# Two transformer layers on one core: some early loads moved to GpSimd's queue, the first products taken by parts, and products of zeros at two places

## The chip, the cores and the metric

The kernel runs on one core of one Trainium2 chip. TensorE (PE) multiplies, VectorE (DVE) and ScalarE (ACT) do the elementwise work, GpSimd (POOL) computes one small power per norm and issues some loads, SyncE (SP) issues nearly all loads. The metric is the device time of one execution in microseconds, the median over several runs.

## The reference

Two layers act on x, 256 rows of 1024 float32 values. A layer is a half-weighted SwiGLU block, a mixer with three kinds of attention, and a second half-weighted SwiGLU block. Each stage begins with an RMS norm, and one more norm ends the program.

```python
for l in range(DEPTH):
    x = x + 0.5 * swiglu(rms_norm(x, ffn1_norm[l]), ffn1_w_gate[l], ffn1_w_up[l], ffn1_w_down[l])
    x = x + hybrid_mixer(rms_norm(x, mix_norm[l]), w_in[l], ...)
    x = x + 0.5 * swiglu(rms_norm(x, ffn2_norm[l]), ffn2_w_gate[l], ffn2_w_up[l], ffn2_w_down[l])
return rms_norm(x, final_norm)
```

D_FF is 2816, so a SwiGLU block reads three matrices of 1024 by 2816 values. Here the stages are called f1_0, mx_0, f2_0, f1_1, mx_1 and f2_1.

## The kernel before, in words

**Products.** Every float32 operand is split into a high and a low part (`split`, `high` on ACT, `low` on DVE), and one product is three matmuls: high by high, low by high, high by low (`mm3`, L173). A weight therefore travels: a load into the raw ring `w_r` (or a tile of its own), a copy by ACT into `w_h`, a subtraction by DVE into `w_l`, then the matmuls.

**The order of the work.** The program's order on PE, ACT and DVE is fixed by hand (`ORDERED`): the code advances a clock of its own (`spend`), defers pieces of work by so many microseconds (`defer`), and `need` runs the deferred pieces until a named one is done. An instruction that waits holds everything behind it on its engine. SP and POOL are not in that list: on them the framework's scheduler places the DMAs, and may take one ahead of another that has to wait.

**Loads.** `load` (L313) starts one load and defers its split. The first block of a SwiGLU stage needs two loads of gate and two of up (512 KB each, columns 0 to 255). Then come single blocks of 128 columns: gate block 2 and up block 2 are the first of them (512 KB each, `128x8x128` in the order's rows). The last 1536 columns are done as two units by Strassen-like products G and U with steps 1, 5, 6, 3, 7, 2, 4; their raw quarters (768 KB each, `128x4x384`, tiles `f_G_r` and `f_U_r`, issued at L322) are called G1, G5, G6, G2 and U1 below after the step that loads them. Some quarters are added to a tile already there by a DMA on POOL's queue (L331).

**The start.** Nine matmuls of zeros into a bank `heat` run first (L1185). Then x's first 128 rows (t=0) are normed: ACT sums squares (L429), POOL takes the power -1/2 (L436), DVE scales (L450), PE transposes, DVE multiplies by the gain (L471), ACT and DVE split the result into `f_Th` and `f_Tl`. `first_block` (L574) multiplies t=0 by gate, then by up, then t=1 by both. `second` loads and norms t=1 meanwhile. `opened` loads the tables `rot` and `tab` (64 and 896 KB), which the mixer reads much later.

**Between stages.** The norm of the next stage works per half of the rows. In f1_1, the products of t=0 run while t=1 is being normed; then PE transposes t=1 (`turn`, L456).

Of the kernel before, what the change touches and what calls it, by code (L numbers as in the profile page):

```python
# [13 lines left out]
ALU = mybir.AluOpType  # L14
# [96 lines left out]
def block_kernel(ctx: ExitStack, tc: tile.TileContext, a: dict, c: dict, out: bass.AP):  # L111
# [57 lines left out]
    def transpose(o, src, n=P):  # L169
        nc.tensor.transpose(o, src, ident[:n, :n])  # L170
        spend(0.11)

    def mm3(o, st, mv, first, last, again=False):  # L173

        (sh, sl), (mh, ml) = st, mv
        nc.tensor.matmul(o, sh, mh, start=first, stop=False, skip_group_check=again)  # L176
        nc.tensor.matmul(o, sl, mh, start=False, stop=False, skip_group_check=again)  # L177
        nc.tensor.matmul(o, sh, ml, start=False, stop=last, skip_group_check=again)  # L178
        spend(3 * (max(256, o.shape[-1]) / 2400 + 0.003))
        load_some()  # L180
        while later and later[0][0] <= clock[0]:
            heapq.heappop(later)[2]()
# [125 lines left out]
        of.append([j])  # L308
        return pool.tile(shape, F32, tag=tag, name=name, bufs=bufs), of[-1]

    unit_pool, unit_open = [None], [False]

    def load(j, ring):  # L313
        job = jobs[j]
        name, n = job["name"], job["n"]
        adds = []
        if "unit" in job:
            places, new, add, source, more = job["unit"]
            if new:
                tag, src = new  # L320
                places[tag] = raw_place("raw" + tag, unit_pool[0], 2 if tag == "a" else 1, [P, 4 * UC], f"{name}_r", j)
                nc.sync.dma_start(places[tag][0].rearrange("p (k n) -> p k n", k=4), src)  # L322
            for t in {source, *(add or ()), *(more or ())[:1]}:
                for i in places[t][1]:
                    if i in loaded:
                        loaded[i][2]()
                if places[t][1][-1] != j:
                    places[t][1].append(j)
            if more:
                tag, src = more  # L330
                nc.gpsimd.dma_start(places[tag][0].rearrange("p (k n) -> p k n", k=4), src, accum_op=ALU.add)  # L331
            raw = places[source][0]
            if add:
                to, other = [places[t][0] for t in add]
                adds = [(to, other)]
        else:
            o, old = take(raws, n, j)
            for i in old:
                loaded[i][2]()
            raw = raws["tile"][:, o:o + n]  # L340
            o = 0
            for w, k0, k1, c0, m in job["runs"]:
                e = o + (k1 - k0) * m
                nc.sync.dma_start(raw[:, o:e].rearrange("p (k n) -> p k n", k=k1 - k0),
                                  w[k0 * P:k1 * P, c0:c0 + m].rearrange("(k p) n -> p k n", p=P))
                o = e
        o, _ = take(rings[ring], n, j)
        hi, lo = [rings[ring][i][:, o:o + n] for i in ("hi", "lo")]
        piece = n // 2 if adds else n if job["whole"] else PIECE
        cuts = [(o, min(n, o + piece)) for o in range(0, n, piece)]  # L350
        todo = [lambda o=o, e=e: nc.vector.tensor_tensor(to[:, o:e], to[:, o:e], other[:, o:e], op=ALU.add)  # L351
                for to, other in adds for o, e in cuts]
        todo += [lambda o=o, e=e: high(hi[:, o:e], raw[:, o:e]) for o, e in cuts]
        todo += [lambda o=o, e=e: low(lo[:, o:e], raw[:, o:e], hi[:, o:e]) for o, e in cuts]
        total = len(todo)

        def until(m):
            while len(todo) > m:
                todo.pop(0)()

        size = piece / 1200 + 0.1
        for m in range(total - 1, -1, -1):
            defer(size * (total - 1 - m), lambda m=m: until(m))
        until(total - 1)
        loaded[j] = hi, lo, lambda: until(0), ring
        return SUM if adds else SPLIT if "unit" in job else PACE * n
# [35 lines left out]
        tl = const.tile([P, KT, S], F32R, tag="xTl", name=f"{name}_Tl")  # L402
        return th, tl

    def norm(name, gain_src, last=None, gain_cols=None):


        st = {}
# [30 lines left out]
        def scaled(t):  # L439
            xs, ss, r = st[t]  # L440
            if last is not None:
                xg = st["xg", t]
                nc.scalar.mul(xg[:, half_cols(0)], xg[:, half_cols(0)], r)
                nc.vector.tensor_scalar(xg[:, half_cols(1)], xg[:, half_cols(1)], r, None, op0=ALU.mult)
                for h in (1, 0):
                    last(t, h, xg)
                return
            for h in range(2):
                if gain_cols is not None:
                    nc.vector.tensor_scalar(xs[:, half_cols(h)], x[t][:, half_cols(h)], r, None, op0=ALU.mult)  # L450
                else:
                    nc.vector.scalar_tensor_tensor(xs[:, half_cols(h)], x[t][:, half_cols(h)], r, st["g"][h], op0=ALU.mult, op1=ALU.mult)
                defer(0.8 + 0.7 * h, lambda h=h: turn(t, h))
            made.add((name, t, "rows"))

        def turn(t, h):  # L456
            tp = tp_bank(f"{name}_tp{t}{h}")
            for k in range(4):
                kk = h * 4 + k
                transpose(tp[:, k, :], st[t][0][:, kk * P:(kk + 1) * P])  # L460
            defer(0.3, lambda: parts_of(t, h, tp))

        def parts_of(t, h, tp):
            th, tl = nT[name]
            src = tp
            if name[0] == "f":
                if h == 0:
                    kept[name, t] = row_tile(f"{name}_xr{t}").rearrange("p (k s) -> p k s", s=P)
                if gain_cols is not None:
                    src = kept[name, t][:, h * 4:h * 4 + 4, :]  # L470
                    nc.vector.tensor_tensor(src, tp, gain_cols[:, h * 4:h * 4 + 4, None].to_broadcast([P, 4, P]), op=ALU.mult)  # L471
                    made.add((name, "kept", t, h))
            split(th[:, h * 4:h * 4 + 4, rows(t)], tl[:, h * 4:h * 4 + 4, rows(t)], src)
            if name[0] == "f" and gain_cols is None:
                defer(1.5, lambda: (nc.scalar.activation(kept[name, t][:, h * 4:h * 4 + 4, :], tp, AF.Copy), made.add((name, "kept", t, h))))
            made.add((name, t, h))
            if t == 1 and h == 1:
                table(AF.Exp if name.startswith("mx") else AF.Silu)
# [52 lines left out]
    def ffn(name, done, opening=None, opened=None):  # L531
        xTh, xTl = nT[name]
        steps, tail, f_first = ffn_steps()
        with ExitStack() as ctx2:
# [24 lines left out]
            def glu(g, u, nm, then, key):  # L559
# [11 lines left out]

                defer(0.25, silu)

            def first_block():  # L574

                pair = hidden(0, 2)
                for t in range(NT):
                    ab = acc_bank(f"{name}_b0{t}").rearrange("p (a b) -> p a b", a=2)
                    for i in range(2):
                        for k in range(KT):  # L580
                            need((name, t, k // 4))
                            mm3(ab[:, i, :], (xTh[:, k, rows(t)], xTl[:, k, rows(t)]), part(f"{name}_{'gu'[i]}0", k),
                                k == 0, k == KT - 1)
                        if opening and t == 0 and i == 0:
                            opening()
                        if t and not i:
                            tps[1], unit_open[0] = True, True
                            sums()
# [6 lines left out]
                                            made.update((name, "hT", i, t) for i in range(2))))  # L595

                    glu(ab[:, 0, :], ab[:, 1, :], f"{name}_b0{t}", lambda h, t=t: defer(2.5, lambda: turn(t, h)), (name, "h", 0, t))
                if opening:
                    opened()

            single = {}

# [120 lines left out]

            first_block()
            for step in steps:
                if step[0] == "P":
                    unit_product(*step[1:])
                elif step[0] == "B":
                    block(*step[1:])
                else:  # L730
                    for t in range(NT):
                        for h in range(2):
                            down(step[1], t, h)
# [8 lines left out]
                        down(f, t, h)  # L742
                    defer(0.2, lambda t=t, h=h: update(t, h))
            need((name, "updated"))
            unit_open[0] = False

    def rows_out(name, st, keys, scale, done):

# [432 lines left out]
    nc.scalar.dma_start(gain_rows, a["ffn1_norm"][0].rearrange("(k p) -> k p", p=P))  # L1181
    nc.scalar.dma_start(ident, c["eye"])
    table(AF.Square)
    heat = acc_bank("heat")
    for _ in range(WARM):  # L1185
        nc.tensor.matmul(heat[:, :256], zeros[:, :P], zeros, start=True, stop=True)
    gain_bank = tp_bank("gain_tp")
    transpose(gain_bank[:, 0, :KT], gain_rows, KT)
    gain_cols = small.tile([P, KT], F32, tag="gc", name="gain_cols", bufs=1)
# [2 lines left out]
    first(0, 0)  # L1192
    first(0, 1)
    need(("f1_0", 0, "rows"))
    load(queues[0].pop(0), 0)
    need(("f1_0", 0, 0), ("f1_0", 0, 1))

    def second():
        x_in(1)
# [5 lines left out]
        pace[0] = clock[0]  # L1205

    def opened():
        nc.sync.dma_start(rot, c["rot"])
        nc.sync.dma_start(tab, c["tab"])

    def write(t, h, rows_):
        (nc.scalar, nc.sync)[h].dma_start(out[0, rows(t), half_cols(h)], rows_[:, half_cols(h)])
# [2 lines left out]
    for i, (kind, l) in enumerate(layers):  # L1215
        if i + 1 < len(layers):
            k2, l2 = layers[i + 1]
            done = norm(f"{k2}_{l2}", a[norms[k2]][l2])
        else:
            done = norm("last", a["final_norm"], last=write)  # L1220
        if kind == "mx":
# [35 lines left out]
```

## Time and profile before

| | |
|---|---|
| median of 3 runs | 1272.26 us (1272.09 to 1272.71) |
| the profiled execution | 1275.12 us, of which the span is 1273.3 us |
| PE busy | 1254.1 us, 98% of the span |
| DVE, ACT, POOL busy | 913.9, 748.1 and 55.6 us |
| HBM read | 244.85 MB, 193 GB/s over the span |

The profiled execution is 2.9 us longer than the median. PE is busy nearly all the time, so the places to read are the few at which it waits, and the stretches in which its clock was granted at half speed (1.2 instead of 2.4 GHz). DMA shares above 1.00 in a stretch occur because a packet's time counts where it starts.

### The profile page before, as it was taken

How to read it: one execution, taken by the hardware profiler on the slowest of the kernel's cores; microseconds unless marked ns; L12 is line 12 of the kernel's file. 1: busy time of each engine (PE TensorE's matmuls, PEld its weight loads, DVE VectorE, ACT ScalarE, POOL GpSimd, SP SyncE). 2: the span in 40 equal slices, each digit the busy share in tenths (PEclk: the TensorE clock that was granted, in tenths of full speed). 3: DMA queues.
4: the chain of work that ended last, by engine and by line, in shares of the span. 5: the costliest groups of instructions: out<-in, count | busy, mean ns of one | idle time of the engine just before them, and what ended most of it. 6: DMA issues, size and time to landing. Idle time of an engine off the chain costs nothing.

```text
span 1273.3 us, 21204 instructions
## 1 busy us (share of the span) xinstructions
PE 1254.1 (98%) x8287; PEld 1178.7 (93%) x8287; DVE 913.9 (72%) x1359; ACT 748.1 (59%) x1263; POOL 55.6 (4%) x54
## 2 busy tenths in 40 slices
PE   7999999999999999999999999999999999999997
PEld 6999988999999899999889999899999998999996
DVE  5988767765546868887688877667655577788774
ACT  5665646655556456665466565467655554665652
POOL 0000001000000000000000000000000000000000
PEclk8999999999999999999999999999999999999999
DMA  9997856545435688986589985565464466799762
GB/s 301 259 263 207 225 189 172 153 131 145 127 111 169 208 256 221 267 229 174 165 261 261 247 239 151 168 178 154 134 165 115 135 198 199 215 267 242 221 167 79
DMA packets 206308, 247.28 MB, mean 194 GB/s; under 512 B 7160, under 2 KB 190208, under 8 KB 206208
## 3 DMA queue, kind: packets, MB, share of 16 engines
q1 hardware_dynamic: 188864, 220.16, 56.1%
q0 software_dynamic: 16896, 25.17, 12.1%
q8 instruction: 65, 1.06, 0.3%
q10 hardware_dynamic: 448, 0.59, 0.1%
q14 instruction: 35, 0.29, 0.1%
HBM read 244.85 MB, written 1.05 MB: 193 GB/s over the span
## 4 chain that ended last, share of the span: by engine, by line
PE 94%; DVE 3%; ACT 1%; DMA 1%; issue 0%; POOL 0%; POOLq 0%; ACTq 0%; DVEq 0%
PE f_a L178 6%; PE f_a L177 6%; PE f_a L176 6%; PE f_s L176 6%; PE f_s L177 6%; PE f_s L178 6%; PE f_b L177 6%; PE f_b L178 6%; PE f_b L176 6%; PE mx_ogate L176 4%; PE mx_ogate L178 3%; PE mx_ogate L177 3%; PE mx_odqk L176 2%; PE mx_odqk L177 2%; PE mx_odqk L178 2%; PE mx_sbdil L846 1%
## 5 line engine op out<-in xcount | busy, mean ns | idle before, releaser
L188 DVE TENSOR_TENSOR w_l<-w_r,w_h 128x512 fp32r<-128x512 f32 (+1 forms) x484 | 386.4, 824 | 96.7 <-ACT w_h L185 95.0
L185 ACT ACTIVATE w_h<-w_r 128x512 fp32r<-128x512 f32 (+1 forms) x484 | 344.3, 734 | 96.6 <-PE f_a L177 16.8
L176 PE MATMUL f_b<-f_Th,w_h 128*128 128x256 f32 x512 | 144.8, 283 | 0.0
L177 PE MATMUL f_b<-f_Th,w_l 128*128 128x256 f32 x512 | 144.6, 282 | 0.0
L178 PE MATMUL f_b<-f_Tl,w_h 128*128 128x256 f32 x512 | 144.6, 282 | 0.0
L178 PE MATMUL f_a<-w_l,f_hTh 128*128 128x512 f32 x352 | 139.8, 397 | 0.0
L176 PE MATMUL f_a<-w_h,f_hTh 128*128 128x512 f32 x352 | 139.1, 395 | 0.0
L177 PE MATMUL f_a<-w_h,f_hTl 128*128 128x512 f32 x352 | 138.7, 394 | 0.0
L188 DVE TENSOR_TENSOR w_l<-f_U_r,w_h 128x1536 fp32r<-128x1536 f32 (+1 forms) x72 | 100.2, 1399 | 33.1 <-ACT w_h L185 31.9
L185 ACT ACTIVATE w_h<-f_G_r 128x1536 fp32r<-128x1536 f32 (+1 forms) x72 | 86.2, 1199 | 46.4 <-DVE f_G_r L351 18.6
L176 PE MATMUL mx_ogate<-mx_Th,w_h 128*128 128x256 f32 x384 | 113.2, 295 | 0.0
L185 ACT ACTIVATE w_h<-f_U_r 128x1536 fp32r<-128x1536 f32 (+1 forms) x72 | 85.7, 1197 | 41.4 <-issue 14.1
L177 PE MATMUL mx_ogate<-mx_Th,w_l 128*128 128x256 f32 x384 | 108.7, 283 | 0.6 <-DVE w_l L188 0.6
L178 PE MATMUL mx_ogate<-mx_Tl,w_h 128*128 128x256 f32 x384 | 108.6, 283 | 0.0
L188 DVE TENSOR_TENSOR w_l<-f_G_r,w_h 128x1536 fp32r<-128x1536 f32 (+1 forms) x72 | 100.0, 1398 | 10.6 <-ACT w_h L185 10.2
L178 PEld LDWEIGHTS f_b<-f_Tl,w_h 128*128 128x128 f32 x512 | 97.9, 191 | 0.0
L177 PEld LDWEIGHTS f_b<-f_Th,w_l 128*128 128x128 f32 x512 | 97.7, 191 | 0.0
L176 PEld LDWEIGHTS f_b<-f_Th,w_h 128*128 128x128 f32 x512 | 97.6, 191 | 0.0
L176 PE MATMUL f_s<-w_h,f_Sh 128*128 128x384 f32 x256 | 87.3, 341 | 0.0
L178 PE MATMUL f_s<-w_l,f_Sh 128*128 128x384 f32 x256 | 86.7, 339 | 0.0
L177 PE MATMUL f_s<-w_h,f_Sl 128*128 128x384 f32 x256 | 86.6, 338 | 0.0
L178 PEld LDWEIGHTS f_a<-w_l,f_hTh 128*128 128x128 f32 x352 | 66.1, 188 | 15.7
(269 smaller groups left out, 2937.3 us busy)
## 6 DMA issues: line engine op xcount, KB each, us to landing
w_r<-in_ffn_w_down SPq DMA_DIRECT2D x88, 512.0 KB, 4.4
w_r<-in_w_in SPq DMA_DIRECT2D x84, 512.0 KB, 3.9
f_G_r<-in_ffn_w_gate SPq DMA_DIRECT2D x32, 768.0 KB, 7.7
f_U_r<-in_ffn_w_up SPq DMA_DIRECT2D x32, 768.0 KB, 8.6
w_r<-in_ffn_w_gate SPq DMA_DIRECT2D x40, 512.0 KB, 6.1
w_r<-in_ffn_w_up SPq DMA_DIRECT2D x40, 512.0 KB, 6.3
f_G_r<-in_ffn_w_gate POOLq DMA_DIRECT2D x16, 768.0 KB, 8.8
f_U_r<-in_ffn_w_up POOLq DMA_DIRECT2D x16, 768.0 KB, 8.4
```

Of the source, the lines that this page charges most:

```text
L176: nc.tensor.matmul(o, sh, mh, start=first, stop=False, skip_group_check=again)
L177: nc.tensor.matmul(o, sl, mh, start=False, stop=False, skip_group_check=again)
L178: nc.tensor.matmul(o, sh, ml, start=False, stop=last, skip_group_check=again)
L185: nc.scalar.activation(hi, src, AF.Copy)
L188: nc.vector.tensor_tensor(lo, src, hi.bitcast(F32), op=ALU.subtract)
L846: nc.tensor.matmul(o if len(k.shape) == 2 else o.rearrange("p (a b) -> p a b", a=NT), q, k, start=True, stop=True)
```

## The change

It has seven parts.

1. The first raw quarter of each SwiGLU stage (G1) is loaded from POOL's queue, not SP's; the tables `rot` and `tab` too.
2. `opened` (the two tables) is called later in the program, at the step that computes G4 of the first unit.
3. The first eight products (t=0 by gate) are taken in two parts of four k each (`by_parts`): the four high by high matmuls, then four with the low half of x, then four with the low half of the weight.
4. For the first norm alone, the second half is transposed sooner (0.1 in place of 0.7), the low part of x is deferred by 1.2, and `kept` is written for all.
5. The split of the first gate load is deferred by 0.9.
6. Three matmuls of zeros after the first transposes, and five in f1_1 before the transposes of t=1 (`warm`).
7. The bank of the zeros comes from `s_bank`, not `acc_bank`.

```diff
+    def warm(n):
+
+        heat = s_bank("heat")
+        for _ in range(n):
+            nc.tensor.matmul(heat[:, :256], zeros[:, :P], zeros, start=True, stop=True)
...
-    unit_pool, unit_open = [None], [False]
+    unit_pool, unit_open = [None], [False, False]
...
-                nc.sync.dma_start(places[tag][0].rearrange("p (k n) -> p k n", k=4), src)
+                (nc.gpsimd if not unit_open[1] else nc.sync).dma_start(places[tag][0].rearrange("p (k n) -> p k n", k=4), src)
+                unit_open[1] = True
...
-                defer(0.8 + 0.7 * h, lambda h=h: turn(t, h))
+                defer(0.8 + (0.7 if gain_cols is None else 0.1) * h, lambda h=h: turn(t, h))
...
         def turn(t, h):
+            if warmed and t == 1 and h == 0:
+                warm(5)
...
+            if gain_cols is not None:
+                src = kept[name, t][:, h * 4:h * 4 + 4, :]
+                nc.vector.tensor_tensor(src, tp, gain_cols[:, h * 4:h * 4 + 4, None].to_broadcast([P, 4, P]), op=ALU.mult)
+                made.add((name, "kept", t, h))
+                high(hi, src)
+                defer(1.2, lambda: (low(lo, src, hi), made.add((name, t, h))))
...
+            def by_parts(o, t, k0):
+
+                ks = range(k0, k0 + 4)
+                w = [part(f"{name}_g0", k) for k in ks]
+                for i, (a, b) in enumerate(((xTh, 0), (xTl, 0), (xTh, 1))):
+                    for k in ks:
+                        nc.tensor.matmul(o, a[:, k, rows(t)], w[k - k0][b], start=k == 0 and i == 0, stop=k == KT - 1 and i == 2)
+                spend(4 * 0.33)
...
+                            if opening and t == 0 and i == 0:
+                                if k % 4 == 0:
+                                    by_parts(ab[:, i, :], t, k)
+                                continue
...
-                if opening:
-                    opened()
...
+                if opening and step == ("P", 0, "G", 4):
+                    opened()
...
-            unit_open[0] = False
+            unit_open[:] = False, False
...
-    heat = acc_bank("heat")
-    for _ in range(WARM):
-        nc.tensor.matmul(heat[:, :256], zeros[:, :P], zeros, start=True, stop=True)
+    warm(WARM)
...
-    load(queues[0].pop(0), 0)
+    defer(0.9, lambda: load(queues[0].pop(0), 0))
     need(("f1_0", 0, 0), ("f1_0", 0, 1))
+    warm(3)
...
-        nc.sync.dma_start(rot, c["rot"])
-        nc.sync.dma_start(tab, c["tab"])
+        nc.gpsimd.dma_start(rot, c["rot"])
+        nc.gpsimd.dma_start(tab, c["tab"])
...
-            done = norm(f"{k2}_{l2}", a[norms[k2]][l2])
+            done = norm(f"{k2}_{l2}", a[norms[k2]][l2], warmed=kind == "f2")
```

The scheduler answers the emptier queue. On SP, at the start of f1_0, the program before has this order (x, the loads of the first block, G1 and the tables, then gate block 2 and up block 2, which are the two rows `128x8x128`):

```order
L216 DMA x_72<-in_x 128x512 x2
L344 DMA w_r<-in_ffn_w_gate 128x4x256 x2
L216 DMA x_73<-in_x 128x512 x2
L344 DMA w_r<-in_ffn_w_up 128x4x256 x2
L322 DMA f_0_G_1_r<-in_ffn_w_gate 128x4x384
L1208 DMA rot<-c_rot 128x128
L1209 DMA tab<-c_tab 128x1792
L344 DMA w_r<-in_ffn_w_gate 128x8x128
L344 DMA w_r<-in_ffn_w_up 128x8x128
L344 DMA w_r<-in_ffn_w_down 128x1024
L322 DMA f_0_G_5_r<-in_ffn_w_gate 128x4x384
```

The changed program has this order there:

```order
L222 DMA x_72<-in_x 128x512 x2
L351 DMA w_r<-in_ffn_w_gate 128x4x256 x2
L222 DMA x_73<-in_x 128x512 x2
L351 DMA w_r<-in_ffn_w_up 128x4x256 x2
L328 DMA f_0_G_5_r<-in_ffn_w_gate 128x4x384
L328 DMA f_0_G_6_r<-in_ffn_w_gate 128x4x384
L328 DMA f_0_G_2_r<-in_ffn_w_gate 128x4x384
L328 DMA f_0_U_1_r<-in_ffn_w_up 128x4x384
L351 DMA w_r<-in_ffn_w_gate 128x8x128
L351 DMA w_r<-in_ffn_w_up 128x8x128
L351 DMA w_r<-in_ffn_w_down 128x1024
```

G1 and the tables have left SP's queue, and four later quarters (G5, G6, G2, U1, 768 KB each) have moved ahead of gate block 2. On POOL, G1, `rot` and `tab` now stand ahead of the first power of the norm (the last two rows; `ISA` belongs to the power):

```order
L328 DMA f_0_G_1_r<-in_ffn_w_gate 128x4x384
L1233 DMA rot<-c_rot 128x128
L1234 DMA tab<-c_tab 128x1792
L443 ISA
L443 TENSOR_TENSOR f_0_r_109<-f_0_ss_108,mhalf 128x1
```

Moving the call of `opened` to a later place in the code has thus not put the tables later on POOL: they wait for nothing, and stand near the front. On ACT, in the first block, the changed program has this order around gate block 2 (the first of the two rows of 128x1024; the three rows of 128x512 ahead of it and the one behind it are the four halves of the up loads; `f_0_Th<-f_0_xr_224` is t=1):

```order
L191 ACTIVATE w_h<-w_r 128x512 x3
L191 ACTIVATE w_h<-w_r 128x1024
L191 ACTIVATE w_h<-w_r 128x512
L191 ACTIVATE f_0_Th<-f_0_xr_224 128x4x128 x2
L202 ACT_TABLE_LOAD
L202 ACTIVATE early<-mhalf 128x2
L191 ACTIVATE w_h<-w_r 128x1024
```

Before, the copy of gate block 2 stood at the same place, ahead of up's last half and of both halves of t=1; only the copy of up block 2 has moved, from between the two halves of t=1 to behind them.

## Rows read from the trace of the kernel before

**Rows 1.** The page's head: the span, busy time by engine, and the DMA engines' busy tenths in 40 slices of the span.

```profile
span 1273.3 us, 21204 instructions
...
PE 1254.1 (98%) x8287; PEld 1178.7 (93%) x8287; DVE 913.9 (72%) x1359; ACT 748.1 (59%) x1263; POOL 55.6 (4%) x54
...
DMA  9997856545435688986589985565464466799762
```

**Rows 2.** PE's waits over the whole program: who waited for what, us in total, times, longest.

```profile
PE f_tp L170 <- DVE f_xs L452: 1.8, 1, 1.8
PE f_b L178 <- DVE w_l L188: 1.8, 2, 0.9
PE f_b L176 <- ACT f_Th L185: 1.5, 2, 1.0
PE f_tp L170 <- DVE f_xs L450: 1.5, 1, 1.5
PE heat L1186 <- DVE zeros L1178: 1.2, 1, 1.2
```

**Rows 3.** The table by stretches: from and to, length, busy time of each engine (instructions), granted clock of PE as a share of full speed, DMA share, GB/s.

```profile
2.00:6.00 4.00, 4.00 (x13) 3.26 (x12) 0.00 (x0) 2.69 (x6) 0.00 (x0) 1.00 0.84 269
11.90:18.70 6.80, 5.71 (x24) 5.14 (x25) 5.43 (x11) 4.46 (x10) 0.55 (x1) 0.50 1.01 346
...
21.60:25.50 3.90, 1.81 (x9) 1.01 (x7) 3.12 (x5) 1.93 (x4) 0.00 (x0) 1.00 0.70 242
25.50:29.00 3.50, 3.45 (x16) 3.45 (x17) 2.80 (x5) 2.61 (x5) 0.00 (x0) 0.51 1.09 358
29.00:40.00 11.00, 11.00 (x92) 11.00 (x92) 10.93 (x16) 8.13 (x12) 1.45 (x1) 1.00 1.00 338
...
647.70:649.70 2.00, 0.17 (x3) 0.07 (x2) 1.56 (x3) 0.25 (x1) 1.03 (x1) 1.00 1.04 379
649.70:653.60 3.90, 3.90 (x21) 3.90 (x22) 2.91 (x4) 1.29 (x3) 0.00 (x0) 0.56 1.11 341
```

**Rows 4.** SP's issues in order of time at the start (start, us taken, line, tile).

```profile
3.90 2.55 SPq L344 DMA_DIRECT2D w_r<-in_ffn_w_up  x2
6.50 1.35 SPq L322 DMA_DIRECT2D f_G_r<-in_ffn_w_gate  x1
7.89 1.72 SPq L1208 DMA_DIRECT2D rot<-c_rot  x1
9.65 0.53 SPq L1209 DMA_DIRECT2D tab<-c_tab  x1
14.95 0.38 SPq L344 DMA_DIRECT2D w_r<-in_ffn_w_gate  x1
16.10 0.38 SPq L344 DMA_DIRECT2D w_r<-in_ffn_w_up  x1
```

**Rows 5.** The DMA view of three short stretches, each with one issue of rows 4 (G1 at 6.50, the table at 9.65, gate block 2 at 14.95): KB, and us from issue to landing.

```profile
f_G_r<-in_ffn_w_gate SPq DMA_DIRECT2D x1, 768.0 KB, 10.0
...
tab<-c_tab SPq DMA_DIRECT2D x1, 896.0 KB, 9.2
...
w_r<-in_ffn_w_gate SPq DMA_DIRECT2D x1, 512.0 KB, 5.6
```

**Rows 6.** Five quarters issued in a row by SP in f2_0: SP's issues, and the DMA view's time to landing of the first (issued at 460.66) and of the last (462.98).

```profile
460.66 2.27 SPq L322 DMA_DIRECT2D f_G_r<-in_ffn_w_gate  x4
462.98 0.83 SPq L322 DMA_DIRECT2D f_U_r<-in_ffn_w_up  x1
...
f_G_r<-in_ffn_w_gate SPq DMA_DIRECT2D x1, 768.0 KB, 4.5
...
f_U_r<-in_ffn_w_up SPq DMA_DIRECT2D x1, 768.0 KB, 10.6
```

**Rows 7.** ACT in order of time at 20 us: the copies of gate block 2 and of up's last half, with the idle time ahead of them and what ended it.

```profile
20.59 1.58 ACT L185 ACTIVATE w_h<-w_r 128x1024 fp32r<-128x1024 f32 x2 [3.23 <-DMA w_r<-in_ffn_w_gate]
```

**Rows 8.** PE in order of time, 22 to 25 us.

```profile
22.23 0.39 PE L176 MATMUL f_b<-w_h,f_Th 128*128 128x256 f32 x1 [0.43 <-ACT w_h L185]
...
24.83 0.38 PE L176 MATMUL f_b<-w_h,f_Th 128*128 128x256 f32 x1 [0.53 <-ACT f_Th L185]
25.55 0.58 PE L177 MATMUL f_b<-w_h,f_Tl 128*128 128x256 f32 x1 [0.34 <-DVE f_Tl L188]
```

**Rows 9.** PE in order of time in f1_1: the transposes of t=1.

```profile
649.66 0.63 PE L170 MATMUL f_tp<-ident,f_xs 128*128 128x128 f32 x4 [1.83 <-DVE f_xs L452]
```

**Rows 10.** The table by stretches for the products of zeros alone (a matmul of zeros is two records).

```profile
5.10:7.20 2.10, 2.10 (x10) 1.55 (x9) 1.00 0.99 331
```

**Rows 11.** The DMA view of 52 to 56 us, by queue (q0 POOL's, q1 SP's): packets, MB, share of 16 engines.

```profile
q0 software_dynamic: 407, 0.63, 88.4%
q1 hardware_dynamic: 403, 0.21, 25.8%
```

**Rows 12.** POOL in order of time: the first power, the first DMA issue, and the power for t=1 in f2_0.

```profile
7.76 0.56 POOL L436 TENSOR_TENSOR f_r<-f_ss,mhalf 128x1 f32<-128x1 f32 x1 [7.31 <-DVE f_ss L435]
...
38.41 1.45 POOL L331 DMA_DIRECT2D f_G_r<-in_ffn_w_gate  x1 [21.63 <-DVE f_G_r L351]
...
462.93 0.56 POOL L436 TENSOR_TENSOR f_r<-f_ss,mhalf 128x1 f32<-128x1 f32 x1 [7.14 <-DVE f_ss L435]
```

More of the change, by code (lines that the diff above doesn't have):

```diff
@@ L403, in transposed, with norm @@
         return th, tl
-    def norm(name, gain_src, last=None, gain_cols=None):
+    def norm(name, gain_src, last=None, gain_cols=None, warmed=False):
         st = {}
@@ L464, in parts_of @@
             th, tl = nT[name]
-            src = tp
-            if name[0] == "f":
[L467 to L474, printed above, removed]
+            hi, lo = [o[:, h * 4:h * 4 + 4, rows(t)] for o in (th, tl)]
+            if name[0] == "f" and h == 0:
+                kept[name, t] = row_tile(f"{name}_xr{t}").rearrange("p (k s) -> p k s", s=P)
+            if gain_cols is not None:
[4 more added lines that the diff above has]
+                defer(1.2, lambda: (low(lo, src, hi), made.add((name, t, h))))
+                if t == 1 and h == 1:
+                    table(AF.Silu)
+                return
+            split(hi, lo, tp)
+            if name[0] == "f":
                 defer(1.5, lambda: (nc.scalar.activation(kept[name, t][:, h * 4:h * 4 + 4, :], tp, AF.Copy), made.add((name, "kept", t, h))))
```

## The prediction

> **What bounds the kernel now.** I read the page's head first: PE is busy 1254.1 of 1273.3 us, so time can come only from PE's waits, from its half-speed stretches, or from a new wait [rows 1]. The view of PE's waits then says where those are: the five largest add up to 7.8 us. Four belong to the first 26 us (the zeros, the first `f_xs` of L450, DVE's `w_l`, ACT's `f_Th`), one of 1.8 us to `f_xs` of L452 in f1_1 [rows 2]. The table by stretches shows the cost around them: from 21.6 to 25.5 us PE works 1.81 of 3.90 us, from 29 on it works all of the time, and right after two of the gaps its clock is at about half (0.51 from 25.5 to 29.0, 0.56 from 649.7 to 653.6) [rows 3]. So any delay of the first block passes whole into the end: behind it PE has no idle time to give back.
>
> What is the first block waiting for? The DMA engines are 84 to 101% busy from 2 us on [rows 3], and the page has them at nine tenths in the first three slices [rows 1]. SP issues gate block 2 at 14.95, after G1 and the tables [rows 4]; it lands 5.6 us later, at 20.6, while the table ahead of it (9.65 + 9.2) landed at 18.9 and G1 (6.50 + 10.0) at 16.5 [rows 5]. The landings keep the order of the issues. At 20.59 ACT, idle for 3.23 us on that very DMA, copies gate block 2, and only behind it the last half of up [rows 7]. PE takes the last up products at 22.23, the first of t=1 at 24.83, and runs without a gap from 25.55 [rows 8]. That is the chain: the landing of gate block 2, a load that the first block doesn't use, plus 5.0 us.
>
> **The change part by part.**
>
> *The start.* In the changed order ACT still copies gate block 2 ahead of up's last half and of t=1, but on SP four quarters of 768 KB now stand ahead of it. One such quarter costs 2.1 us of the DMA engines: in f2_0 five in a row land from 465.2 (460.66 + 4.5) to 473.6 (462.98 + 10.6), four intervals in 8.4 us [rows 6]. The last up load landed about one quarter before G1, at 16.5 - 2.1 = 14.4. Gate block 2 itself takes 20.6 - 18.9 = 1.7. So:
>
> - If POOL's three loads cost SP's nothing, gate block 2 lands at 14.4 + 4 x 2.1 + 1.7 = 24.5, which is 3.9 late.
> - If they take from SP's loads what they took in SP's own queue (18.9 - 14.4 = 4.5), it lands at 29.0, 8.4 late.
> - I take 28.4, 7.8 late, since from 2 to 6 us the DMA share was 0.84 [rows 3], and POOL's loads can use these 4 x 0.16 = 0.6 us of the engines.
>
> The value lies near the second bound because of [rows 11]: with both queues active, POOL's moved 0.63 MB and SP's 0.21 MB in 4 us. SP's loads did not go on beside POOL's at their 346 GB/s [rows 3], they lost most of it. The Trainium skill (page Trainium Kernel Development and Optimization, Key Constraints) has a rule against this part of the change: DMAs issued from SP, ACT and POOL run on the same 16 DMA engines and interleave, and issuing from several saves issue time alone. By that rule the second bound holds and the sum would be +6.9; without it, the first, and +2.4.
>
> The shift goes through the same 5.0 us as before, so PE runs without a gap from about 33.4 in place of 25.55. **Term: +7.8 (3.9 to 8.4; 13.4 in a rival below).** The half-speed stretch behind the gap is there in both [rows 3]; I count no difference.
>
> *What happens before that wait costs or gives nothing.* ACT's changed order puts the first half of x ahead of the gate's copy; the first eight products go by parts; three matmuls of zeros run six passes of 2.10/10 = 0.21 us [rows 10], 1.3 us, where PE has nothing else. They could keep the clock up: 11.9 to 18.7 ran at 0.50 with 5.71 us busy [rows 3], so up to 2.9 us of PE time. But whatever PE finishes earlier, it then waits longer for gate block 2. The cover is about ten microseconds of PE's waiting; without it this group is worth -2.9 to +0.6 (ACT's copy behind the first half of x).
>
> *POOL.* The three issues stand ahead of the first power. At the longest issue seen, 1.45 us [rows 12], they end near 0.7 + 3 x 1.45 = 5.1, before the power's 7.76 [rows 12]: nothing. If they were held up, x would come late into the same cover. In f2_0, f1_1 and f2_1 G1 stands on POOL between the powers for t=0 and t=1. SP issued it at 460.66 in f2_0, the power came at 462.93 [rows 6, 12]; less 1.45 for the issue, 0.8 us are to spare. I count 0, at most 0.9 each if the issue waits longer than on SP. The bytes are the same.
>
> *f1_1.* Five matmuls of zeros are ten passes of 0.21, 2.1 us, in a gap of 1.83 [rows 9, 10]; they overrun it by 0.2 to 0.3. In return the stretch from 649.7 to 653.6 may keep full speed: at 0.56 of it, 3.9 us would take 3.9 x 0.56 = 2.2, a gain of 1.7 [rows 3]. **Term: -1.5** (from -1.7 to +0.3, the last if the clock would not have fallen there, or falls anyway).
>
> **Sum.** +7.8 - 1.5 = +6.3. Against the profiled execution's 1275.1 that is 1281.4; that execution stands 2.9 above the median, so on the median of 1272.3 it gives **1278.6 us**, 0.5% slower. One measurement of this kernel can tell about 0.2%, 2.5 us, from no change.
>
> **The rivals.**
>
> *Faster: gate block 2 does not wait behind the quarters.* If its packets went through the engines ahead of G5 to U1, it could land as early as 14.4 + 1.7 = 16.1, 4.5 us sooner than before, with G1 and the tables out of SP's way. Then the change does what its words say: 1272.3 - 4.5 - 1.5 = 1266.3. The point that decides is the landing at 20.6 + 1.5 = 22.1: below it the kernel is faster. For it: the queue holds loads of different shapes, and I infer order from landings alone. Against it: all landings of [rows 5, 6] came in the order of issue, gate block 2 among them behind a table of 896 KB. The Trainium skill (page DMA: Bandwidth & Descriptors, Queues, rings and completion order) says that completion isn't first in, first out per issuing engine, but that each DMA engine consumes descriptors in ring order; the trace agrees with the latter. Chance 0.11.
>
> *No change: the two queues fit together.* If the engines had room for POOL's three loads (768 + 64 + 896 KB, 1.77 MB) beside SP's, the term is its lower bound: +3.9 - 1.5 = +2.4, 1274.7. Against it: the shares near 1.00 [rows 3]. Chance 0.09.
>
> *Slower still: the mixed stretch is inefficient.* In [rows 11] both queues together moved 0.84 MB in 4 us, 210 GB/s. At that rate POOL's 1.77 MB take 1.77/0.158 = 11.2 us, in which SP's queue moves 0.59 MB in place of 3.88 at 346 GB/s: 3.29 MB, or 9.5 us, late in place of 4.5. Then gate block 2 lands at 24.5 + 9.5 = 34.0, 13.4 late, and the time is 1272.3 + 13.4 - 1.5 = 1284.2. Against it: the transfers in those rows add to a tile, these three only write. Chance 0.10.
>
> **How the numbers follow.** The forecast, with its own spread of 1276 to 1281, has 0.70, the rivals 0.11, 0.09 and 0.10. Slower by over 0.2% are the forecast and the last rival, 0.80; within 0.2% is the second, 0.09; faster is the first, 0.11. The range reaches from the edge of the second rival to the last, 1274.0 to 1284.5; left out are the first rival and the tails.
>
> **What would show it.** In the changed profile SP should issue four quarters before gate block 2, and it should land near 28. ACT should wait some ten microseconds for it, PE should be idle for most of 18 to 29 us and take the first product of t=1 near 32.6. POOL's queue should show traffic from about 3 us. In f1_1 the gap of 1.83 should be filled with zeros, and the granted clock stay at 1.00. The forecast is wrong if gate block 2 lands before 22, or if ACT copies up's last half without it; the size is wrong if it lands far from 28, which tells how the two queues share the engines.

## The result: slower by 9.0 us

The changed kernel takes 1281.32 us (1280.85 to 1283.18, 6 runs), the kernel before beside it 1272.28 (1272.09 to 1272.89, 6 runs): ratio 1.0072, 95% interval 1.0062 to 1.0083. The cause is the one forecast, the size is 2.7 us over the forecast's +6.3. The profiled executions differ by 8.1 us (1283.18 and 1275.12); why that is not 9.0 is taken up below.

### The profile page after: what moved, and what is told of

Its sections match the earlier page's. It is cut to its first block, busy times and chain, and to the rows that moved or that the text cites. A ratio compares the mean times of both kernels' runs of the same rounds, so it can differ in the third digit from the quotient of the medians.

```text
span 1281.4 us, 21237 instructions
## 1 busy us (share of the span) xinstructions
PE 1256.9 (98%) x8303; PEld 1181.0 (92%) x8303; DVE 913.4 (71%) x1359; ACT 748.0 (58%) x1263; POOL 59.4 (5%) x60
## 4 chain that ended last, share of the span: by engine, by line
PE 94%; DMA 2%; DVE 2%; ACT 1%; issue 0%; POOL 0%; SPq 0%; POOLq 0%; DVEq 0%; ACTq 0%
PE f_a L184 6%; PE f_a L183 6%; PE f_a L182 6%; PE f_s L182 6%; PE f_s L184 6%; PE f_s L183 6%; PE f_b L183 6%; PE f_b L184 6%; PE f_b L182 6%; PE mx_ogate L182 4%; PE mx_ogate L184 3%; PE mx_ogate L183 3%; DMA w_r<-in_ffn_w_gate 2%; PE mx_odqk L182 2%; PE mx_odqk L184 2%; PE mx_odqk L183 2%
```

## The profile after

The page's head, to be held against [rows 1]: the span, busy time, PE's clock and the DMA tenths.

```profile
span 1281.4 us, 21237 instructions
...
PE 1256.9 (98%) x8303; PEld 1181.0 (92%) x8303; DVE 913.4 (71%) x1359; ACT 748.0 (58%) x1263; POOL 59.4 (5%) x60
...
PEclk8899999999999999999999999999999999999999
DMA  9698865555544587987579986565454466799762
```

PE is busy 2.8 us more (the eight added matmuls of zeros alone take 1.46 and 2.32), and the span is 8.1 longer: 5.3 are new waiting. PE's waits (who, for what, us in total, times, longest), to be held against [rows 2]:

```profile
PE f_b L182 <- ACT w_h L191: 7.6, 1, 7.6
PE f_b L593 <- ACT w_h L191: 2.8, 2, 2.3
PE f_tp L170 <- DVE f_xs L457: 1.5, 1, 1.5
```

One wait of 7.6 us is new, a smaller one of 2.8 too, ahead of the first products by parts (L593), and the 1.8 of f1_1 is gone. What is ACT late with in the long one? SP's issues in order of time (start, us taken, line, tile), to be held against [rows 4], and below them the DMA view of four short stretches (KB, us from issue to landing): the last up load, G5, U1 and gate block 2.

```profile
3.79 6.18 SPq L351 DMA_DIRECT2D w_r<-in_ffn_w_up  x2
10.01 5.89 SPq L328 DMA_DIRECT2D f_G_r<-in_ffn_w_gate  x3
15.94 1.42 SPq L328 DMA_DIRECT2D f_U_r<-in_ffn_w_up  x1
17.48 1.73 SPq L351 DMA_DIRECT2D w_r<-in_ffn_w_gate  x1
```

```profile
w_r<-in_ffn_w_up SPq DMA_DIRECT2D x1, 512.0 KB, 13.8
...
f_G_r<-in_ffn_w_gate SPq DMA_DIRECT2D x1, 768.0 KB, 10.8
...
f_U_r<-in_ffn_w_up SPq DMA_DIRECT2D x1, 768.0 KB, 11.2
...
w_r<-in_ffn_w_gate SPq DMA_DIRECT2D x1, 512.0 KB, 11.4
```

The four quarters stand ahead of gate block 2. The second of the two up loads was issued at 4.88 and lands 13.8 later, at 18.7. G5 lands at 10.01 + 10.8 = 20.8 and U1 at 15.94 + 11.2 = 27.1, so three intervals take 6.3, 2.1 each. Gate block 2 lands at 17.48 + 11.4 = 28.9. ACT in order of time (us in brackets: idle before it, and what ended that), then PE:

```profile
28.94 1.58 ACT L191 ACTIVATE w_h<-w_r 128x1024 fp32r<-128x1024 f32 x2 [9.09 <-DMA w_r<-in_ffn_w_gate]
32.49 1.23 ACT L191 ACTIVATE f_Th<-f_xr 128x512 fp32r<-128x512 f32 x2 [1.97 <-DVE f_xr L479]
```

```profile
30.57 0.58 PE L182 MATMUL f_b<-w_h,f_Th 128*128 128x256 f32 x1 [7.61 <-ACT w_h L191]
...
33.17 0.58 PE L182 MATMUL f_b<-w_h,f_Th 128*128 128x256 f32 x1
33.90 0.58 PE L183 MATMUL f_b<-w_h,f_Tl 128*128 128x256 f32 x1
```

ACT idles 9.09 us on a transfer that the first block does not use, as in [rows 7] with 3.23. Up's last half landed at 18.7, ten microseconds before ACT came to copy it, and PE waits for that copy. From the landing to PE without a gap it is 33.90 - 28.9 = 5.0, as before.

The table by stretches (from and to, length, busy time and instructions of PE, PEld, DVE, ACT, POOL, granted clock, DMA share, GB/s), to be held against [rows 3]:

```profile
15.20:18.60 3.40, 3.40 (x19) 3.40 (x18) 2.53 (x7) 2.22 (x6) 0.55 (x1) 0.50 1.08 362
18.60:25.50 6.90, 4.14 (x29) 3.37 (x28) 1.82 (x3) 1.15 (x2) 0.00 (x0) 0.99 1.07 367
25.50:30.50 5.00, 0.00 (x0) 0.00 (x0) 0.47 (x1) 1.56 (x2) 0.00 (x0) 0.50 1.14 327
30.50:33.20 2.70, 2.05 (x7) 1.46 (x7) 2.60 (x5) 0.73 (x3) 0.00 (x0) 0.50 0.35 128
33.20:39.10 5.90, 5.76 (x25) 5.46 (x26) 4.09 (x6) 4.55 (x6) 0.00 (x0) 0.50 0.94 223
39.10:50.00 10.90, 10.90 (x89) 10.90 (x88) 10.70 (x15) 7.36 (x13) 1.35 (x1) 1.00 0.29 93
...
657.30:661.20 3.90, 3.90 (x29) 3.65 (x28) 3.43 (x6) 1.29 (x3) 0.57 (x1) 1.00 1.02 329
```

Behind the wait PE works at half speed until 39.1, 5.76 us of work, where it was 3.45 before. In f1_1 the clock stays at 1.00; PE in order of time there, to be held against [rows 9]:

```profile
656.79 2.32 PE L177 MATMUL heat<-zeros 128*128 128x256 f32 x10
658.95 0.60 PE L170 MATMUL f_tp<-ident,f_xs 128*128 128x128 f32 x4
```

Last, the DMA view from 5 to 10 us by queue (q0 is POOL's, q1 SP's: packets, MB, share of 16 engines), to be held against [rows 11]:

```profile
DMA packets 706, 1.84 MB, mean 367 GB/s; under 512 B 41, under 2 KB 436, under 8 KB 706
...
q0 software_dynamic: 303, 1.43, 73.9%
q1 hardware_dynamic: 403, 0.40, 24.5%
```

Both queues get packets through in like numbers, but POOL's are 4.7 KB each and SP's 1.0 KB, so POOL's loads take three quarters of the engines from the very loads the first block waits for. It is clearest from 7 to 10 us, where both queues are busy all the time:

```profile
q0 software_dynamic: 200, 0.97, 83.1%
q1 hardware_dynamic: 207, 0.21, 19.8%
```

[rows 11] had shown it: 407 packets and 403, 0.63 MB and 0.21. The Trainium skill (page DMA: Bandwidth & Descriptors, Queues, rings and completion order) says that each DMA engine goes round the queues by whole packets; the trace agrees, with 200 and 207 packets. No run altered the size of the packets.

## The experiments

Ratios are to the kernel before, run on the same chip. The landing is that of gate block 2.

| run | median us | ratio, 95% interval | landing |
|---|---|---|---|
| the change | 1281.32 | 1.0072 (1.0062 to 1.0083) | 28.9 |
| e1, the queue alone | 1284.23 | 1.0082 (1.0067 to 1.0097) | 28.9 |
| e2, all but the queue | 1270.72 | 0.9980 (0.9970 to 0.9989) | 18.4 |
| e3, ACT's copy later | 1274.95 | 1.0013 (1.0004 to 1.0022) | 29.0 |
| e8, SP in order | 1273.23 | 1.0000 (0.9990 to 1.0010) | 20.5 |
| e9, and tables late | 1270.81 | 0.9978 (0.9969 to 0.9987) | 17.8 |
| e10, and G1 on SP | 1270.30 | 0.9976 (0.9966 to 0.9986) | 17.6 |
| e12, and copy later | 1269.22 | 0.9974 (0.9963 to 0.9984) | 17.4 |
| e5, zeros of f1_1 alone | 1272.38 | 0.9991 (0.9982 to 1.0000) | 20.1 |
| e13, before in order, zeros | 1271.29 | 0.9989 (0.9981 to 0.9998) | 20.1 |
| e6, zeros in the wait | 1282.54 | 1.0072 (1.0058 to 1.0085) | 29.3 |
| e7, zeros in all gaps | 1282.30 | 1.0075 (1.0060 to 1.0090) | 29.0 |
| e14, fewer, G1 back | 1281.31 | 1.0070 (1.0056 to 1.0084) | 28.8 |

**e1 and e2: which part costs.** e1 is the kernel before with parts 1 and 2, e2 the change without them. The cut shows e2's lines against the change (`opened` is also called at its old place again):

```diff
-                (nc.gpsimd if not unit_open[1] else nc.sync).dma_start(places[tag][0]...
+                nc.sync.dma_start(places[tag][0]...
-        nc.gpsimd.dma_start(rot, c["rot"])
-        nc.gpsimd.dma_start(tab, c["tab"])
+        nc.sync.dma_start(rot, c["rot"])
+        nc.sync.dma_start(tab, c["tab"])
```

> The kernel before with parts 1 and 2 alone: G1 and both tables go from GpSimd's queue, the tables are called for later; products, ACT's order and zeros stay as before. The scheduler again puts the four later quarters ahead of gate block 2 on SP, and one mixer load of 512 KB more. Theory (gate block 2, stuck behind the quarters and beside POOL's loads, sets the end): it lands near 30.3 in place of 20.6, ACT waits for it as long as in the change, PE runs without a gap 9 to 11 us later, and without the gain in f1_1 the time is 1281.5 to 1284. Rival (the products by parts, ACT's new order or the zeros cost the time): within 1.5 of the kernel before, 1271 to 1274.

> The change without parts 1 and 2: G1 and the tables are on SP's queue again and called for at their old place; products by parts, ACT's order and both sets of zeros stay. On SP only G1 and the small table now stand ahead of gate block 2, the large table behind it. Theory: gate block 2 lands near 18.3, 2.3 before the kernel before; with the 1.3 of f1_1 that is 1268.5 to 1271. Rival (by parts, order or zeros cost the time): 1278 to 1282.

The two split the change: the queue alone costs 10.4 us (by the ratio), the rest alone gains 2.5. Together that is 7.9, within the intervals the change's 9.0. e1's median lies 0.2 over its range, its landing 1.4 before the one expected. In e1 ACT waits as in the change:

```profile
28.88 1.58 ACT L185 ACTIVATE w_h<-w_r 128x1024 fp32r<-128x1024 f32 x2 [9.30 <-DMA w_r<-in_ffn_w_gate]
```

**e3: does the late transfer cost, or the copy's place?** One number is altered, the clock at which the later splits may start:

```diff
-        pace[0] = clock[0]
+        pace[0] = clock[0] + 5.5
```

> The change with one number altered: the clock by which the loads behind the first are split starts 5.5 us later, so that ACT copies up's last half and splits t=1 ahead of gate block 2; SP's and POOL's queues stay as in the change, with the four quarters ahead. Theory (the late transfer costs time only because ACT's copy of it stands ahead of work that the first block needs): the wait of 7.6 us at the first block goes, PE waits for gate block 2 only behind the first block, by about 2 us less than the block takes, and the time is 1273 to 1277. Rival (the start is bound by the transfers however the copies stand): gate block 2 still lands at 28.9, PE is without a gap from 33.9 as in the change, and the time is 1280 to 1282.

The transfers are as late as in the change, and of its 9.0 us 6.4 (medians) to 7.5 (ratios) are gone. ACT in e3, in order of time:

```profile
17.37 1.67 ACT L191 ACTIVATE w_h<-w_r 128x512 fp32r<-128x512 f32 x3 [0.87 <-DMA w_r<-in_ffn_w_up]
21.50 0.63 ACT L191 ACTIVATE f_Th<-f_xr 128x512 fp32r<-128x512 f32 x1 [2.45 <-DVE f_xr L479]
...
29.02 1.06 ACT L191 ACTIVATE w_h<-w_r 128x1024 fp32r<-128x1024 f32 x1 [4.25 <-DMA w_r<-in_ffn_w_gate]
```

Up's last half is copied at 17.4 and t=1 split at 21.5; ACT waits for gate block 2 only behind that, when PE still has products.

**e8, e9, e10: the quarters, the tables, G1.** They build on each other: SP's DMAs in the order of the program; then two elements of each table written by DVE where the tables are called for, so that their loads come there; then G1 on SP's queue.

```diff
-ORDERED = {mybir.EngineType.PE, mybir.EngineType.Activation, mybir.EngineType.DVE}
+ORDERED = {mybir.EngineType.PE, mybir.EngineType.Activation, mybir.EngineType.DVE, mybir.EngineType.SP}
...
+        nc.vector.memset(rot[:, 0, 0, :2], 0.0)
+        nc.vector.memset(tab[:, :2], 0.0)
...
-                (nc.gpsimd if not unit_open[1] else nc.sync).dma_start(places[tag][0]...
+                nc.sync.dma_start(places[tag][0]...
```

> The change with SP's DMAs in the order of the program, so that gate block 2 and up block 2 stand ahead of the four quarters; G1 and the tables go from GpSimd's queue at the start as in the change, with the same bytes and beside SP's loads. Theory (the quarters ahead are the larger part of the delay, POOL's loads beside SP's the smaller): gate block 2 lands near 20.4, as before, and the time is 1269.5 to 1272 with the gain in f1_1. Rival (GpSimd's queue alone is what delays SP's loads): gate block 2 lands at 24 or later, and the time is 1275 or more.

> The kernel with SP's DMAs in the order of the program (gate block 2 ahead of the quarters), with one addition: VectorE writes two elements of each table at the later place at which the tables are called for, so GpSimd's loads of them really come there; at the start GpSimd loads G1 alone. Theory (each byte that GpSimd's queue moves at the start delays SP's loads by what it takes of the DMA engines): gate block 2 lands 2.6 earlier than with the tables at the start, near 17.8, and the time is 1.5 to 2.6 less, 1270.6 to 1271.7. Rival (beside SP's loads POOL's cost nothing): no difference in landing or time.

> As with the tables late and SP in the order of the program, but G1 too is on SP's queue again, behind up block 2: ahead of gate block 2 there are only the loads that the first block needs, and GpSimd's queue is empty at the start. Theory: gate block 2 lands near 16.1, 1.7 earlier than with G1 on GpSimd's queue; ACT and DVE then set the start of t=1, so of these 1.7 at least half shows: 1269 to 1271. Rival (G1 on GpSimd's queue costs SP's loads nothing): no difference from the run with the tables late.

e8's landing came out as expected (20.5; ACT's line is below), so POOL's loads alone do not make the delay; its time is 1.2 over the range. The expectation had left out the gate loads, which POOL's three delay too. The second line is PE in e8, waiting for the first product by parts, which in e10 starts at 11.76 after 0.23:

```profile
20.47 1.58 ACT L191 ACTIVATE w_h<-w_r 128x1024 fp32r<-128x1024 f32 x2 [0.55 <-DMA w_r<-in_ffn_w_gate]
...
13.96 0.51 PE L593 MATMUL f_b<-w_h,f_Th 128*128 128x256 f32 x2 [2.35 <-ACT w_h L191]
```

e9 is as expected: without the tables the landing comes at 17.8, and the time is 2.4 less. The Trainium skill (page Trainium Kernel Development and Optimization, Key Constraints) says that another issuing engine saves issue time alone. For the tables (896 and 64 KB) the run agrees that nothing else is saved; SP's issue time wasn't saved either, its two up loads took 6.36 us to issue in e8 and 3.23 in e9. For G1 the runs don't decide: 0.5 less in e10, inside both intervals. Its landing at 17.6 in place of 16.1 was my oversight. SP's waits in e10 from 0 to 20 us:

```profile
SPq L351 <- DVE w_l L194: 7.1, 2, 5.1
```

Gate block 2 goes into a raw tile that DVE must first have read, and SP can't issue it before 13.75, whatever stands in the queue.

**e12: the best of these, with the copy later.**

```diff
-        pace[0] = clock[0]
+        pace[0] = clock[0] + 3.0
```

> The run with an empty GpSimd queue at the start, SP in the order of the program and the tables late, with one number altered: the splits behind the first loads start 3.0 us later by the kernel's own clock, so that ACT and VectorE split up's last half and t=1 ahead of gate block 2. There t=1's products waited on VectorE's row of gate block 2 and up's last half. Theory (the copy's place still costs about 2 us of them): t=1 starts near 20 in place of 21.8, and the time is 1268 to 1269.5, against 1270.3. Rival (what is saved there is waited for behind the first block, at gate block 2 itself): 1270 to 1271.

The median is in the theory's range, 1.1 under e10; the ratios differ by 0.0002 only (the two ran beside other runs of the kernel before), so whether it beats e10 is open. It beats the kernel before by 0.26% (0.16 to 0.37) and the change by 12 us. ACT in e12 has the four up copies in one, and t=1 at 19.60, in e10 at 21.13:

```profile
14.72 2.17 ACT L191 ACTIVATE w_h<-w_r 128x512 fp32r<-128x512 f32 x4
19.60 1.23 ACT L191 ACTIVATE f_Th<-f_xr 128x512 fp32r<-128x512 f32 x2 [2.70 <-DVE f_xr L479]
```

**e5: the zeros of f1_1 alone; e13: what the parts at the start are worth without the cover.** e5 adds `warm(5)` in f1_1 to the kernel before. e13 adds SP's order to e5 (the first two lines of the diff above), so that it differs from e10 by parts 3 to 7 at the start, and in where the tables are loaded.

```diff
+            if warmed and t == 1 and h == 0:
+                warm(5)
```

> The kernel before with the five matmuls of zeros in f1_1 alone. Theory (they fill the gap, and the half-speed stretch from 650 goes with it): the gap of 1.83 us ahead of the transposes goes, the clock stays at 1.00 there, and the time is 1.3 us less (0.5 to 1.7). Rival (the zeros only overrun the gap, or the clock falls all the same): 0.3 more to 0.3 less.

> The kernel before with two things: SP's DMAs in the order of the program, and the five matmuls of zeros in f1_1. SP's loads then stand as in the best run of the change's kind (gate block 2 and up block 2 ahead of G1), but the products by parts, ACT's order and the three zeros at the start are not there. Theory (without the long wait that covered them these three parts are worth something: the clock at the start): half speed from about 12 to 19 stays, and the time is 1271 to 1273, 1 to 2.5 over the run with them at 1270.3. Rival (they are worth nothing with the cover gone either): 1269.8 to 1270.8.

e5 is 1.1 faster by either measure, with the interval touching 1. SP's order by itself is worth little in the kernel before: e13 stands 0.2 (ratios) to 1.1 (medians) under e5, so what e8 gained on the change is the quarters' doing. e13 stands 1.0 (medians) to 1.6 (ratios) over e10, but the two intervals overlap. A stretch in the table of e13, then one of e10:

```profile
14.20:21.00 6.80, 5.27 (x26) 4.99 (x25) 5.25 (x10) 5.25 (x11) 0.55 (x1) 0.50 0.54 149
```

```profile
5.20:27.00 21.80, 17.36 (x119) 15.25 (x118) 15.41 (x27) 13.53 (x24) 1.11 (x2) 1.00 0.87 285
```

With the cover gone these parts are worth something, as far as one may read it from overlapping intervals and from kernels that load the tables at different places: in the profiled executions e10 has full speed all along, e13 half speed for 6.8 us, and gate block 2 is issued at 16.09 in place of 13.75, since its raw tile comes free later.

**e6, e7, e14: is half speed behind the wait the missing 2.7 us?** e6 puts 17 matmuls of zeros ahead of the fifth product of up (the wait stands ahead of the seventh, 30.57 above; the zeros fill it all the same), e7 five more into the gaps behind it; e14 takes 14, 2 and 1, and G1 on POOL in f1_0 alone. The cut shows e14's lines.

```diff
+                            if opening and i == 1 - t and k in (0, 4, 6):
+                                warm({(0, 4): 14, (0, 6): 2, (1, 0): 1}.get((t, k), 0))
...
-                (nc.gpsimd if not unit_open[1] else nc.sync).dma_start(places[tag][0]...
+                (nc.gpsimd if name[:4] == "f1_0" and not unit_open[1] else nc.sync).dma_start(places[tag][0]...
```

> The change with 17 matmuls of zeros added on PE between the fourth and the fifth product of up for t=0, where PE waits 7.6 us; by 2 x 0.21 each they take 7.1 us at full speed. Nothing else is altered. Theory (the 2.7 us that the forecast fell short are mostly the longer half-speed stretch behind this wait, 13.7 us in place of 3.4, 5.2 of them with PE at work): PE starts t=1 at the same 33.2, keeps 1.00 there, and the time falls by 2.0 to 2.9, to 1278.4 to 1279.3. Rival (the half-speed stretch is no part of the size): the time stays within 0.7 of the change.

> The change with 17 matmuls of zeros in the wait of 7.6 us, as in the run before, and five more in the gaps that were left behind it: 3 ahead of the seventh product of up for t=0, 2 ahead of t=1's first product. With 17 alone the clock held through the wait, then fell at 33.4, behind gaps of 0.27, 0.84 and 0.53, for 6.8 us. Theory (half speed behind the wait is the part of the size that the forecast missed): with these gaps filled the clock stays at 1.00 up to the end, and the time is 2.0 to 3.0 under the change, 1278.3 to 1279.3. Rival (half speed there costs nothing, or the clock falls whatever PE does): within 0.8 of the change.

> The change with zeros in the waits of the first block once more, but fewer (14, 2 and 1 matmuls in place of 17, 3 and 2, since those overran the waits and t=1 began 1.36 later), and with G1 on SP's queue in the stages behind the first (in f2_0, with G1 on GpSimd's queue and PE 1.2 earlier, ACT waited 1.6 for G1 and the 1.2 were lost). The queues at the start are those of the change. Theory (half speed behind the wait costs 2.6, which the run before did win and then lost to these two): t=1 begins near 33.3, the clock holds, f2_0 loses nothing, and the time is 1.8 to 2.8 under the change's 1281.3: 1278.5 to 1279.5. Rival (the 2.6 are lost somewhere else too): 1280.5 to 1282.

All three missed their theory: the medians of e6 and e7 are 1.2 and 1.0 over the change's, and e14's is the same as the change's (its rival had 1280.5 to 1282). The tables by stretches, of e6, of e7, and of e14:

```profile
33.40:40.20 6.80, 6.52 (x29) 6.23 (x30) 4.87 (x9) 4.87 (x7) 0.00 (x0) 0.50 0.86 236
```

```profile
21.10:24.50 3.40, 3.40 (x15) 3.13 (x14) 0.15 (x1) 0.00 (x0) 0.00 (x0) 0.50 1.06 372
33.40:40.20 6.80, 6.80 (x57) 6.70 (x55) 4.96 (x8) 5.99 (x8) 0.00 (x0) 1.00 0.89 255
```

```profile
33.40:40.20 6.80, 6.46 (x55) 6.44 (x55) 4.96 (x8) 5.88 (x10) 0.00 (x0) 1.00 0.86 249
```

In e6 the clock held through the zeros and fell behind the gaps that were left. In e7 and e14 it holds from 33.4 on: PE does 57 and 55 instructions in the 6.8 us, e6 29. But e7's zeros ran partly at half speed themselves and overran; t=1 began at 34.53. In f2_0 ACT then waited for G1, which comes from POOL's queue there:

```profile
479.45 1.49 ACT L191 ACTIVATE w_h<-f_G_r 128x1536 fp32r<-128x1536 f32 x1 [1.62 <-DMA f_G_r<-in_ffn_w_gate]
```

e14 has neither fault, and its profiled execution is 1.6 under the change's profiled one (1281.57 and 1283.18). But it has a third. The last product ahead of PE's transposes of the first block's result starts 2.4 earlier than in the change (44.27 and 46.67). Then these transposes wait for DVE, where in the change they followed at once (46.79):

```profile
45.28 0.44 PE L170 MATMUL f_b0tp<-ident,f_f_b_h 128*128 128x128 f32 x2 [0.74 <-DVE f_f_b_h L581]
```

So full speed gave PE 2.4 us there, and about 1.5 of them stayed: half speed had hidden a wait on DVE. e14's median, though, is the change's. So in the executions that I can see full speed is worth some 1.6 us, and nothing in the median. The runs of the change spread from 1280.85 to 1283.18, and whether those at 1281 have the long half-speed stretch no trace shows; the section below has what their mean clocks say.

## Why the prediction was right, and where its size was off

- **The number: partly luck.** 1281.32 lies 0.3 over the forecast's own spread of 1276 to 1281. It is inside the whole range because that reaches up to the rival of the inefficient mix, and nothing of that rival came true.
- **Cause: shown.** The queue's part costs all of it (e1, e2). Step by step from e10: G1 on POOL 0.5, the tables on POOL at the start 2.4, the four quarters ahead of gate block 2 8.1 (medians of e10, e9, e8, the change: 1270.3, 1270.8, 1273.2, 1281.3; by the ratios 0.3, 2.8 and 9.2). The copy's place on ACT is what turns most of the late transfer into time (e3: 6.4 to 7.5 of the 9.0).
- **Landing of gate block 2, 28.4: found 28.9.** The quarters are 2.1 each and gate block 2 1.8 (2.1 and 1.7 in the working); up's last load came at 18.7, where the working had 14.4 + 3.9 = 18.3. The 0.6 us of room left to POOL's loads was really 0.2. So its reason, that POOL's queue takes most of the engines, was right; that this is a matter of packet sizes I had not read from [rows 11].
- **5.0 us from the landing to PE without a gap:** 5.0 again.
- **"The half-speed stretch behind the gap is there in both, I count no difference": the step that failed.** Behind the point from which PE runs without a gap it is 5.2 us (33.9 to 39.1), not 3.45; at half speed the difference costs (5.2 - 3.45)/2 = 0.9.
- **f1_1, -1.5:** the gap and the half-speed stretch went, the zeros overran as forecast. The traces give -1.4 (below), e5 measures -1.1 (-2.3 to 0).
- **By parts, ACT's order, three zeros: nothing under the wait.** e1 with e5 gives 1.0082 - 0.0009 = 1.0073, the change with all parts 1.0072; the intervals leave room for 2 us either way. Without the cover they gain 1.0 to 1.6, within the -2.9 to +0.6 of the text.
- **POOL's issues and G1 on POOL, 0:** right. At the start POOL has issued all three by 3.4, long before the power at 7.72. In f2_0 the cover is thin: the change has 0.3 us of waiting on ACT and none on PE, but e7, 1.2 us ahead of the change there, lost 1.0 of it. The issue and the power of the change's start:

```profile
1.31 0.94 POOL L328 DMA_DIRECT2D f_G_r<-in_ffn_w_gate  x1 [0.86 <-POOLq L1264]
...
7.72 0.56 POOL L443 TENSOR_TENSOR f_r<-f_ss,mhalf 128x1 f32<-128x1 f32 x1 [4.36 <-DVE f_ss L442]
```

- **A reading:** the working has the DMA engines 84 to 101% busy from 2 us on, but [rows 3] has 0.70 from 21.6 to 25.5 us. No term used that stretch.

**The 2.7 us.** In the profiled pair they can be followed along PE, by the first product of the first unit and PE's last matmul, before and after:

```profile
38.94 0.34 PE L176 MATMUL f_s<-w_h,f_Th 128*128 128x384 f32 x1
48.08 0.34 PE L182 MATMUL f_s<-w_h,f_Th 128*128 128x384 f32 x1
...
1266.44 0.40 PE L178 MATMUL f_a<-w_l,f_hTh 128*128 128x512 f32 x1
1274.13 0.40 PE L184 MATMUL f_a<-w_l,f_hTh 128*128 128x512 f32 x1
```

Behind the first block PE is 9.1 late: 8.35 of it are there when PE runs without a gap (33.90 - 25.55), 0.8 come with half speed. At the end it is 7.7 late, so f1_1 gave back 1.4; and from there to the span's end it takes 0.4 more (7.3 and 6.9). That makes 9.1 - 1.4 + 0.4 = 8.1, the difference of the profiled pair, where the forecast had 7.8 - 1.5 = 6.3. The last 1.0 is between profiles and medians: I set before's execution 2.9 over its median and took that for the change as well, whose profiled one is 1.9 over. The execution of e5, whose start is that of the kernel before, has no half speed behind the gap (its table by stretches):

```profile
25.50:29.00 3.50, 3.20 (x26) 3.00 (x26) 2.80 (x5) 3.28 (x5) 0.00 (x0) 1.00 0.97 237
```

So executions of the same instructions can differ in this stretch, against the 0.51 of [rows 3]; the two also differ in the landing (20.1 and 20.6) and in where the half speed ahead of it lies (13.3 to 20.1 and 11.9 to 18.7). The record has the mean granted clock of every execution. Of the kernel before, 13 executions have 0.994, as the profiled one, and took 1274.5 to 1275.3; 14 have 0.997 and took 1271.0 to 1273.0. The change's profiled one has 0.992, its three at 0.994 took 1281.2 to 1281.3, and its two at 0.993 1280.9 and 1282.3. So both profiled executions have more half speed than those near the medians. Where the others have it, and so whether half speed or something else makes the last microsecond of the medians, stays open; e14, at 0.997 and 0.998, is no faster in the median than the change.

**The rivals.** Faster: no, gate block 2 landed far behind 22.1; the landings kept the order of SP's issues. No change: no, the engines had no room for POOL's loads. Slower still by an inefficient mix: no, both queues together moved 367 GB/s from 5 to 10 us, against the 210 of [rows 11].

## What to carry to other kernels

Before loads are taken out of a queue, look at what the scheduler pulls into the hole: here four loads of later use went ahead of one that a fixed order on another engine was waiting for, which cost 8 to 9 us where the loads moved away cost 3. A second queue is no second lane; look at the packets and bytes of each queue while both are busy, and be wary of loads of large packets at the time in which small ones are needed (argued from the packet counts; what was run is moving such loads to later, e9). Either pin the order of the load queue together with the compute engines', or put the copy of a load no earlier than the work that really needs it: here either alone took back 6 us or more of the 9.

## What was not expected of the hardware

- Two queues shared the DMA engines by packets, not by bytes: 200 and 207 packets, 0.97 and 0.21 MB from 7 to 10 us.
- With POOL's queue busy, SP's own issue of the two up loads took 6.18 us; before, 2.55 [rows 4]. It was 4.68 to 6.43 in the other runs with all three loads on POOL (e1, e3, e6, e7, e8, e14), 3.23 with G1 alone (e9) and 1.63 to 2.69 with none (e2, e5, e10, e12, e13). So what stands behind on SP is issued late as well; why, no run shows.
- In e6 the clock held through 7.5 us of zeros and then fell to half for 6.8 us behind gaps of 0.27, 0.84 and 0.53. In e7, with all gaps filled, it held; in e14 it held too, though gaps of 0.83 and 0.34 were left.
